# A two-layer conv/attention trunk: weight slots that mix blocks, vector work paced by counted time, every turn through DRAM

## The chip, the cores and the metric

One core of a Trainium2 chip runs one program. The metric is the device time of one execution in microseconds, as the median of several runs. PE is TensorE, DVE VectorE, ACT ScalarE, POOL GpSimd, SP SyncE; SP and POOL only issue DMAs here, apart from a few memsets.

## The reference

Two layers with the same structure on 256 positions of width 2048, all in float32. A layer norms x, multiplies it by one wide matrix, and splits the product between two branches; each branch is gated and projected, and the sum goes through an output projection onto x.

```python
def hybrid_layer(x, cos, sin, norm_g, w_in, ...):
    h = rmsnorm(x, norm_g)
    proj = h @ w_in
    (c_a, c_glu, c_gate, q_down, kv_down, k_pe, m_gate, g_conv, g_mla) = jnp.split(proj, idx, axis=-1)
    y_conv = conv_branch(c_a, c_glu, c_gate, conv_w, conv_b, conv_ln_g, conv_ln_b) @ w_proj_conv
    y_mla = mla_branch(q_down, kv_down, k_pe, m_gate, cos, sin, ...) @ w_proj_mla
    y = jax.nn.sigmoid(g_conv) * y_conv + jax.nn.sigmoid(g_mla) * y_mla
    return x + y @ w_out
```

The convolution branch is c_a * sigmoid(c_glu), a causal convolution of 31 taps in each of the 2048 channels, a layer norm over the channels, and two SiLU gates. The attention branch expands q_down and kv_down (512 wide) to 16 heads of 192 for queries and keys (128 plain, 64 rotated) and 128 for values, norms queries and keys per head, and attends with a mask of chunks of 64.

## The kernel before

**Products.** Every projection is cut into blocks of up to 512 output columns. `product` (line 289) runs a block as a row of slots. A slot takes one piece of weights, 2 x 128 input channels, and issues 12 matmuls: for both halves of the positions and both chunks, high x high, low x high and high x low, all fp32r, so that two rounded parts stand for one float32. SP loads a piece as `raw` (line 183), ACT rounds it to `hi` (line 194), DVE subtracts to get `lo` (line 210); `raw` has 5 buffers, `hi` 4, `lo` 3. A block of w_in has 8 slots, one of the query or key expansion (`uq`, `ukv`) 2. The results lie in `acc`, four banks of PSUM, two for each block that runs. They are evacuated one slot after the block's end (`EVAC_AT`).

**The order.** `order_of_layer` (line 89) lists a layer's blocks: a first gated block `glu`, the three blocks `down`, two more `glu`; then for each of 8 pairs of heads `uq`, `ukv` and one more `glu` or gate block; then the gates, the projections `pmla` and `pconv`, and `wout`. A block runs to its end before the next one starts. Everything else is placed against the running slot: `at_slot(n, f)` (line 223) issues f behind the n-th slot from now, and `late` behind the other work of the slot. The statistics, turns, scores, exponentials and values of a pair hang on `ukv` at fixed slots (lines 67 and 68: scores at 17, values at 32). `InOrder` (line 119) keeps each engine's instructions in the order of the calls.

**Fill.** The convolution's taps and its layer norm lie in a queue, `fill`. Behind each slot `background` (line 242) adds to a budget for DVE and ACT what the slot's matmuls leave beside the split, takes off the cost written beside each placed task, and issues fill while DVE's budget is positive. A tap is one addition of 128x512 where ACT has scaled the input beforehand (`scale`, line 839), else two multiply-adds of 128x256 (line 850). The costs are written by hand, such as `costs = (0.62, 0.0)`.

**Turns.** To move channels to the partitions, a block is written to DRAM in four parts by POOL (`park`, line 321), read back (`fetch`) four slots later, and transposed in squares of 32 by DVE at the eighth (`turn`, line 338). Only the last quarter of `pconv`, and of `wout` before another layer, is transposed by PE with an identity into the PSUM tile `tp` (`turn4`, line 986), as the next product needs it soon.

**The other PE work.** The scores `s` of a pair are 16 matmuls, the values `o_ps` 12 (line 781). The layer norm's mean `mu` and variance `var` are sums over the partitions by matmuls of plain F32 with a matrix of 1/2048 (lines 890 and 912); `mu` is issued a slot after the last tap was issued. The pair's statistics end in `rsqrt_steps` (line 369), a run of dependent instructions of 8 elements.

Of the kernel before, what the change touches and what calls it, by code (L numbers as in the profile page):

```python
# [12 lines left out]
F32 = mybir.dt.float32  # L13
# [7 lines left out]
P = 128  # L21
T = 2
# [35 lines left out]
KS = 2  # L58
N_WARM = 9
# [7 lines left out]
STATS_AT, SCALE_AT, QK_BACK_AT, QK_TURN_AT, NOPE_AT, ROPE_AT, SCORES_AT = 2, 3, 6, 11, 12, 14, 17  # L67
MAX_AT, EXP_AT, P_BACK_AT, P_TURN_AT, P_SPLIT_AT, VALUES_AT, O_AT = 18, 19, 23, 28, 30, 32, 34
# [20 lines left out]
def order_of_layer():  # L89

    order = [("glu", 0, "win")] + [("down", i, "win") for i in range(len(DOWN_BLOCKS))]
    order += [("glu", 1, "win"), ("glu", 2, "win")]
    for b in range(NPAIR):
        order += [("uq", b, "wuq"), ("ukv", b, "wukv")]
        if b + 3 < 8:
            order.append(("glu", b + 3, "win"))
        elif b + 1 < NPAIR:
            order.append(("cgate", b - 5, "win"))
    for kind, s in (
        ("cgate", "win"), ("mgate", "win"), ("gmla", "win"), ("pmla", "wpm"),  # L100
        ("gconv", "win"), ("pconv", "wpc"), ("wout", "wo"),
    ):
        order += [(kind, i, s) for i in range(2 if kind == "cgate" else 0, 4)]
    return order

# [10 lines left out]
def trunk(ctx: ExitStack, tc: tile.TileContext, xT, x, g_in, pos, win, wuq, wukv, wpc, wpm, wo, cst, rows, invf, out):  # L116
    nc = tc.nc

    class InOrder:


        def __init__(self, engine):
            self.engine, self.last = engine, None

        def __getattr__(self, name):
            def issue(*a, **k):
# [4 lines left out]
                self.last = ins.ins  # L131
                return ins
# [3 lines left out]
    pe, vec, act, gps, sp = (InOrder(e) for e in (nc.tensor, nc.vector, nc.scalar, nc.gpsimd, nc.sync))  # L136
# [14 lines left out]
    acc_p = pool("acc", 4, space=PSUM)  # L151
    tp_p = pool("tp", 2, space=PSUM)
# [5 lines left out]
    streams = {"win": (win, 16), "wuq": (wuq, 4), "wukv": (wukv, 4), "wpc": (wpc, 16), "wpm": (wpm, 16), "wo": (wo, 16)}  # L158
    taken = {}
    pieces = []  # L160

    def plan(layer, stream):
        ap, nk = streams[stream]
        i, at = taken.get((layer, stream), (0, 0))
        n = blocks_of_layer()[stream][i]
        mine = []
        for g in range(nk // KS):
            size = P * KS * n
            pieces.append((ap[layer, at : at + size].rearrange("(p k c) -> p k c", p=P, k=KS), n))
            at += size  # L170
            mine.append(len(pieces) - 1)
        taken[layer, stream] = (i + 1, at)
        return nk, n, mine


    plans = []
    for l in range(DEPTH):
        plans.append([(k, i, plan(l, s)) for k, i, s in order_of_layer()])
# [42 lines left out]
    fill, budget, marks, owed, assist = deque(), {"vec": 0.0, "act": 0.0}, {}, [], []  # L221

    def at_slot(ahead, f, vec=0.0, act=0.0):
        steps.append((clock[0] + ahead, (vec, act), f))

    def spend(costs):
        budget["vec"] -= costs[0]
        budget["act"] -= costs[1]

    def soon(f, vec=0.0, act=0.0):  # L230

        owed.append(f)
        at_slot(1, lambda: pay(f), vec, act)
# [8 lines left out]
    def background(n):  # L242
        clock[0] += 1
        slot = 12 * (n / 2400 + 0.0133) - 0.04
        for e, split_us in (("vec", KS * n / 960 + 0.06), ("act", KS * n / 1066 + 0.04)):
            budget[e] = min(budget[e], 0.0) + slot - split_us
        while True:
# [4 lines left out]
            for _, costs, f in due:  # L252
                spend(costs)
                f()
# [1037 lines left out]
```

## Time and profile before

| | |
|---|---|
| median of 3 runs | 1903.43 us (1903.39 to 1903.7) |
| span of the profiled execution | 1900.7 us, 2.7 below the median; its own time from outside was not recorded |
| busy PE / DVE / ACT / POOL | 99% / 84% / 70% / 21% |
| DMA | 441.91 MB, 232 GB/s in the mean |

How to read it: a row of groups gives line, engine, operation, out<-in, shape, count, then busy time, mean ns of one, and the idle time ahead of it with what ended it. All instructions go through one helper and show its line (L127), so tiles tell them apart. A row of waits gives who waited for whom, the total, the count and the longest. The chain of waits, followed back from the end, is shown in order of time. PE's busy time counts pipelined matmuls to their modelled ends, so the distance of starts is the better measure of their rate.

### The profile page before, as it was taken

Reading aid. Unit: us, or ns where it says so; the run is one execution under the profiler, and the core shown is the slowest. Engines: PE = TensorE matmul, PEld = TensorE weight load, DVE = VectorE, ACT = ScalarE, POOL = GpSimd, SP = SyncE. Lnnn points to the kernel's source line nnn. Section 1 sums busy time; section 2 is a strip of 40 time slices with the busy share of each in tenths; the row PEclk is TensorE's granted clock in tenths of the full one; section 3 lists DMA queues with packets and bytes.
Section 4 is the critical chain, followed back from the end, with each engine's and each line's share of the span. In section 5 each row is a group of like instructions: output and inputs, shape, how many; then the busy total and the mean of one; then the engine's idle time right before and its main releaser. Section 6 shows DMA issues by size and latency. Waiting matters only on the chain.

```text
span 1900.7 us, 27392 instructions
## 1 busy us (share of the span) xinstructions
PE 1886.3 (99%) x8753; PEld 1591.4 (84%) x8753; DVE 1601.6 (84%) x2620; ACT 1329.3 (70%) x2346; POOL 394.3 (21%) x734
## 2 busy tenths in 40 slices
PE   9999999999999999999999999999999999999999
PEld 7988888888888878888899888888888888788887
DVE  6899888899999998565669898988999999975654
ACT  6677887878788757444557688688887887574442
POOL 0143433332200000121211443343322000001200
PEclk9999999999999999999999999999999999999999
DMA  8777778776765566577866787887777555656764
GB/s 296 233 246 259 255 243 273 264 253 216 239 210 186 186 215 216 203 238 256 286 211 214 254 270 242 262 267 240 261 226 237 199 184 196 221 200 214 240 223 164
DMA packets 137376, 441.91 MB, mean 232 GB/s; under 512 B 23440, under 2 KB 27280, under 8 KB 137232
## 3 DMA queue, kind: packets, MB, share of 16 engines
q1 hardware_dynamic: 104688, 359.50, 55.3%
q0 software_dynamic: 31968, 80.26, 13.4%
q8 instruction: 68, 1.11, 0.2%
q14 instruction: 76, 0.62, 0.1%
q10 hardware_dynamic: 576, 0.41, 0.1%
HBM read 397.61 MB, written 42.47 MB: 232 GB/s over the span
## 4 chain that ended last, share of the span: by engine, by line
PE 94%; DVE 2%; DMA 1%; issue 1%; ACT 1%; SPq 0%; POOL 0%; DVEq 0%; ACTq 0%
PE acc L127 91%; PE s L127 2%; PE o_ps L127 1%; DVE lo L127 1%; DVE v_t L127 1%; DMA raw<-in_win 1%; DMA pos_t<-in_pos 0%; ACT hi L127 0%; SPq L127 0%; DVE qk L127 0%; PE tp L127 0%; DVE rsq_t L127 0%; DMA turn_d<-pr 0%; PE mu L127 0%; ACT junk L127 0%
## 5 line engine op out<-in xcount | busy, mean ns | idle before, releaser
L127 DVE TENSOR_TENSOR lo<-raw,hi 128x1024 fp32r<-128x1024 f32 (+3 forms) x689 | 812.3, 1182 | 214.9 <-PE acc L127 173.0
L127 ACT CAST hi<-raw 128x1024 fp32r<-128x1024 f32 (+3 forms) x689 | 699.3, 1022 | 413.1 <-PE acc L127 343.1
L127 PE MATMUL acc<-hi,hT 128*128 128x512 f32 (+2 forms) x1728 | 419.8, 382 | 0.0
L127 PEld LDWEIGHTS acc<-hi,hT 128*128 128x128 f32 x1728 | 319.7, 188 | 59.2
L127 ACT ACTIVATE tap<-u_t,cst 128x256 f32<-128x256 f32 x594 | 259.7, 500 | 20.5 <-DVE v_t L127 19.8
L127 PE MATMUL acc<-hi,h_hi 128*128 128x512 f32 (+2 forms) x864 | 261.6, 384 | 0.7 <-ACT hi L127 0.7
L127 PE MATMUL acc<-hi,h_lo 128*128 128x512 f32 (+2 forms) x864 | 261.1, 383 | 0.0
L127 PE MATMUL acc<-lo,h_hi 128*128 128x512 f32 (+2 forms) x864 | 230.4, 383 | 2.4 <-DVE lo L127 2.4
L127 PE MATMUL acc<-lo,hT 128*128 128x512 f32 (+2 forms) x864 | 229.3, 382 | 0.0
L127 DVE TENSOR_TENSOR v_t<-v_t,tap 128x512 f32<-128x512 f32 x297 | 204.2, 688 | 10.6 <-ACT tap L127 0.5
L127 PEld LDWEIGHTS acc<-lo,h_hi 128*128 128x128 f32 x864 | 160.8, 188 | 33.1 <-DVE lo L127 3.1
L127 PEld LDWEIGHTS acc<-hi,h_lo 128*128 128x128 f32 x864 | 161.7, 188 | 30.1
L127 PEld LDWEIGHTS acc<-hi,h_hi 128*128 128x128 f32 x864 | 160.8, 188 | 30.9 <-ACT hi L127 1.8
L127 PEld LDWEIGHTS acc<-lo,hT 128*128 128x128 f32 x864 | 160.5, 188 | 29.9
L127 POOL DMA_DIRECT2D turn_d<-gate x176 | 95.9, 553 | 342.9 <-DVE gate L127 298.6
L127 DVE SCALAR_TENSOR_TENSOR v_t<-u_t,cst,v_t 128x256 f32<-128x256 f32 x366 | 157.9, 481 | 3.2
L127 POOL DMA_DIRECT2D turned<-turn_d x82 | 46.0, 562 | 502.9 <-DVE v_t L127 162.4
L127 PE MATMUL acc<-hi,oT 128*128 128x512 f32 x512 | 128.1, 390 | 0.0
L127 PE MATMUL acc<-hi,yT 128*128 128x512 f32 x512 | 128.0, 389 | 0.0
L127 PE MATMUL acc<-hi,ycT 128*128 128x512 f32 x512 | 127.7, 389 | 0.0
L127 PE MATMUL acc<-hi,qkc 128*128 128x512 f32 (+1 forms) x512 | 119.1, 364 | 1.4 <-ACT junk L127 1.4
L127 PEld LDWEIGHTS acc<-hi,oT 128*128 128x128 f32 x512 | 96.1, 188 | 20.2
(166 smaller groups left out, 2143.8 us busy)
## 6 DMA issues: line engine op xcount, KB each, us to landing
raw<-in_win SPq DMA_DIRECT2D x383, 512.0 KB, 4.2
raw<-in_wpm SPq DMA_DIRECT2D x64, 512.0 KB, 3.2
raw<-in_wpc SPq DMA_DIRECT2D x64, 512.0 KB, 3.7
raw<-in_wo SPq DMA_DIRECT2D x64, 512.0 KB, 4.3
raw<-in_wukv SPq DMA_DIRECT2D x32, 512.0 KB, 5.3
turned<-turn_d POOLq DMA_DIRECT2D x50, 256.0 KB, 4.4
raw<-in_win SPq DMA_DIRECT2D x32, 384.0 KB, 4.5
raw<-in_wuq SPq DMA_DIRECT2D x32, 384.0 KB, 3.0
```

What stands on the lines that cost most here:

```text
L127: ins = getattr(self.engine, name)(*a, **k)
```

## The change

1. **Slots that mix blocks.** `slots_of_layer` lists single slots: each `uq` and `ukv` (2 slots each) stands inside a gate block (3 slots of it, `uq`, 2 slots, `ukv`, 3 slots). Blocks 0 and 1 of `pconv` and `wout`, and in layer 1 the first `glu` with the first `down`, run in turns of two slots. Weight pieces are loaded in that order. PSUM has two fixed pairs of banks, handed on when a block ends.
2. **Pace by counted time.** The budgets and hand-written costs go. Every instruction issued on PE, DVE and ACT adds a time by its shape to a counter; at each slot the counters of DVE and ACT are raised to PE's, and fill runs while DVE's is over 0.4 us behind PE's.
3. **Turns by DRAM alone.** `turn4`, the identity and `tp` go.
4. **PE work.** The values take high and low part of the probabilities in one matmul of 512 columns, and end in two banks that ACT copies and DVE adds. Mean and variance first add their two halves, split the sum into two fp32r parts, and take two matmuls.
5. **DVE and ACT.** Small steps of the statistics are woven between large DVE instructions. Taps by addition and the sum `s1` are split in two halves. The gate's first factor is scaled by ACT, and the product issued a slot later. Several `late` tasks move a slot on.
6. **Places.** Scores at 20, values at 34; the rope tables compute five slots later, and their loads come one slot earlier; the first `mgate` tile is turned 6 slots after its evacuation, the last `cgate` tile is parked 2 slots later; x for `wout` is loaded three slots before a block's end. The first chunk of x and the gains come as one tile.

```diff
+STREAM_K = {"win": NCT, "wuq": LORA // P, "wukv": LORA // P, "wpc": NCT, "wpm": NCT, "wo": NCT}
...
-STATS_AT, SCALE_AT, QK_BACK_AT, QK_TURN_AT, NOPE_AT, ROPE_AT, SCORES_AT = 2, 3, 6, 11, 12, 14, 17
-MAX_AT, EXP_AT, P_BACK_AT, P_TURN_AT, P_SPLIT_AT, VALUES_AT, O_AT = 18, 19, 23, 28, 30, 32, 34
+STATS_AT, SCALE_AT, QK_BACK_AT, QK_TURN_AT, NOPE_AT, ROPE_AT, SCORES_AT = 2, 5, 9, 14, 15, 17, 20
+MAX_AT, EXP_AT, P_BACK_AT, P_TURN_AT, P_SPLIT_AT, VALUES_AT, O_AT = 21, 22, 25, 28, 31, 34, 36
...
+        if kind in ("pconv", "wout") and i == 0 or layer and kind == "glu" and i == 0:
+            for j in range(0, slots[b], 2):
+                out += [(b + a, j + e) for a in range(2) for e in range(2)]
+            b += 2
+        elif b + 1 < len(order) and order[b + 1][0] == "uq":
+            out += [(b, 0), (b, 1), (b, 2), (b + 1, 0), (b + 1, 1), (b, 3), (b, 4), (b + 2, 0), (b + 2, 1)]
+            out += [(b, 5), (b, 6), (b, 7)]
+            b += 3
...
+    now = {"pe": 0.0, "vec": 0.0, "act": 0.0}
+    def pe_us(name, dst, lhs, rhs, **_):
+        return (rhs.free_size() + 32) / 2400
+    def vec_us(name, dst, *a, **_):
+        if name == "tensor_copy":
+            return dst.free_size() / 1920 + 0.08
+        n = dst.free_size() if name != "tensor_reduce" else a[0].free_size()
+        if n <= 8:
+            return 0.19
+        return n / 960 + (0.13 if name == "scalar_tensor_tensor" and not isinstance(a[1], float) else 0.07)
...
+    def weave(dst):
+        if woven and not weaving and dst.shape[0] == P and dst.free_size() >= 128:
+            weaving.append(1)
+            if next(woven[0], woven) is woven:
+                woven.popleft()
+            weaving.pop()
+    vec.after = weave
...
-        while fill and budget["vec"] > 0:
+        while fill and now["vec"] < now["pe"] - 0.4:
             after, slots, scalar = fill[0][1]
-            if after and clock[0] < marks.get(after, 1 << 30) + slots or scalar and budget["act"] < 0:
+            if any(clock[0] < marks.get(a, 1 << 30) + slots for a in after) or scalar and now["act"] > now["pe"]:
                 break
             run_fill()
-        while assist and budget["act"] > 0.8 and assist[0]():
-            budget["act"] -= 0.85
+        while assist and now["act"] < now["pe"] - 0.8 and assist[0]():
+            pass
...
+        for e in ("vec", "act"):
+            now[e] = max(now[e], now["pe"])
...
             def values():
-                st["o"] = tp_p.tile([P, 2, SEQ], F32, tag="tp", name="o_ps")
+                st["o"] = o_p.tile([P, 2, 2, SEQ], F32, tag="o", name="o_ps")
...
+                    pe.matmul(o, v[0][:, 0, h, :], A.pt[:, :, h, past], start=True, stop=False)
+                    pe.matmul(o[:, 0, P:], v[1][:, 1, h, :], A.pt[:, 0, h, own], start=False, stop=False)
+                    pe.matmul(o[:, 0, :], v[1][:, 0, h, :], A.pt[:, 0, h, past], start=False, stop=False)
+                    pe.matmul(o[:, :, P:], v[0][:, 1, h, :], A.pt[:, :, h, own], start=False, stop=True)
...
+                act.copy(o, st["o"][:, :, 0, :])
+                at_slot(1, lambda: vec.tensor_add(o, st["o"][:, :, 1, :], o))
...
+            act.activation(u, ps[:, :256], AF.Copy, scale=r)
...
-                vec.scalar_tensor_tensor(u, ps[:, :256], r, sg, op0=ALU.mult, op1=ALU.mult)
+                vec.tensor_mul(u, u, sg)
...
-                    vec.tensor_add(v[:, :, :SEQ], v[:, :, :SEQ], scaled.pop(k))
+                        vec.tensor_add(vj, vj, own[:, j])
...
-                for j in range(2):
-                    pe.matmul(st["mu"], ones, s1[:, j, :], start=j == 0, stop=j == 1)
+                    for n, part in enumerate(st["parts"]):
+                        pe.matmul(st[name], ones, part, start=n == 0, stop=n == 1)
...
-            then(mean, after=("s1", 7), slots=1)
+            then(mean_sum, after=(("s1", 7),))
+            then(mean, after=(("mean", "parts"),), slots=2)
...
-            if c < 3:
-                return turn(src, 512, None, then=use, then_costs=costs)
...
-                    pe.transpose(tps[0][:, j].rearrange("p i s -> p (i s)"), src[:, j * P : (j + 1) * P], ident)
...
-            turn4(evac_src, c, use, 0.65, 0.65)
+            turn(evac_src, 512, None, then=use)
...
-            late.append(normalised)
+            at_slot(1 if c else 6, normalised)
...
-                        at_slot(a + 2, lambda: next(tables, None), 0.0 if a < 2 else 0.95)
+                        at_slot(a + (1 if a < 2 else 7), lambda: next(tables, None))
...
+            if blk.kind == "wout" and j == blk.nk // KS - 3:
+                wout_begin(blk.i)
```

Three places show what moves. PE, the values of the first pair in layer 0, before; `pv` holds the probabilities and values as they are split, `qk_t` more of the same.

```order
L127 MATMUL o_ps<-pv_1402 128x256
L127 MATMUL o_ps<-pv_1402 128x128 x3
L127 MATMUL o_ps<-pv_1402 128x256 x3
L127 MATMUL o_ps<-pv_1402 128x128 x3
L127 MATMUL o_ps<-pv_1402 128x256 x2
```

PE at the same place now.

```order
L169 MATMUL o_ps<-pv_1523 128x512
L169 MATMUL o_ps<-pv_1523 128x128
L169 MATMUL o_ps<-pv_1523 128x256
L169 MATMUL o_ps<-pv_1523 128x2x128
L169 MATMUL o_ps<-pv_1523 128x512
L169 MATMUL o_ps<-pv_1523 128x128
L169 MATMUL o_ps<-pv_1523 128x256
L169 MATMUL o_ps<-pv_1523 128x2x128
```

Twelve matmuls of 2304 columns in all have become eight of 2304.

DVE, the statistics of a pair of layer 0, before: `ss_p` sums of squares, `r_p` the factors, `rsq_t` a helper.

```order
L127 TENSOR_TENSOR lo_3123<-raw_2963,hi_3087 128x1024
L127 TENSOR_TENSOR ss_p<-ss_p,ss_d 128x4
L127 TENSOR_SCALAR ms<-ss_p 128x8
L127 TENSOR_SCALAR rsq_t<-ms 128x8
L127 TENSOR_SCALAR r_p<-rsq_t 128x8
L127 TENSOR_TENSOR rsq_t<-r_p 128x8
L127 SCALAR_TENSOR_TENSOR rsq_t<-rsq_t,ms 128x8
L127 SCALAR_TENSOR_TENSOR r_p<-rsq_t,r_p 128x8
```

DVE at the statistics of the same pair now.

```order
L169 TENSOR_TENSOR ss_p<-ss_p,ss_d 128x4
L169 SCALAR_TENSOR_TENSOR v_t<-u_t,cst,v_t 128x256
L169 TENSOR_SCALAR ms<-ss_p 128x8
L169 SCALAR_TENSOR_TENSOR v_t<-u_t,cst,v_t 128x256
L169 TENSOR_SCALAR rsq_t<-ms 128x8
L169 TENSOR_TENSOR lo_3381<-raw_3248,hi_3354 128x1024
L169 TENSOR_SCALAR r_p<-rsq_t 128x8
L169 RECIPROCAL rinv<-sums 128x2x2
L169 STREAM_TRANSPOSE pr<-pr 128x768
L169 TENSOR_TENSOR rsq_t<-r_p 128x8
```

The dependent small steps, one run before, now stand one by one behind large instructions; the rest of the run follows closed up, ahead of the scaling of the keys.

PE, the mean of layer 1, before: the two matmuls of `mu` follow the slot of `lo_16312`.

```order
L127 MATMUL acc_0_16290<-lo_16312,oT_14461 128x512 x2
L127 MATMUL acc_1_16291<-lo_16312,oT_14461 128x512 x2
L127 MATMUL mu<-s1c,ones 128x256 x2
L127 MATMUL acc_0_16290<-hi_16314,oT_14461 128x512 x2
L127 MATMUL acc_0_16290<-hi_16314,oT_14462 128x512 x2
```

DVE at that place, before: the last tap and `s1c` stand behind `lo_16337`, which belongs to the slot after it.

```order
L127 TENSOR_TENSOR lo_16312<-raw_16185,hi_16294 128x1024
L127 TENSOR_TENSOR v_t<-v_t,tap 128x2x256 x2
L127 SCALAR_TENSOR_TENSOR v_t<-u_t,cst,v_t 128x256 x2
L127 TENSOR_TENSOR lo_16337<-raw_16212,hi_16314 128x1024
L127 TENSOR_TENSOR v_t<-v_t,tap 128x2x256
L127 TENSOR_TENSOR s1c<-s1c,v_t 128x512
```

DVE there now: the sum's low half `tot` stands behind `lo_16898`, and PE takes `mean` behind the slot of `lo_16898`.

```order
L169 TENSOR_TENSOR s1c<-s1c,v_t 128x256 x2
L169 TENSOR_TENSOR lo_16838<-raw_16713,hi_16818 128x1024
L169 STREAM_TRANSPOSE turned<-turned 128x512 x2
L169 TENSOR_TENSOR lo_16858<-raw_16747,hi_16840 128x1024
L169 TENSOR_TENSOR ln_stats<-s1c 128x256
L169 TENSOR_TENSOR lo_16877<-raw_16767,hi_16860 128x1024
L169 TENSOR_TENSOR lo_16898<-raw_16795,hi_16879 128x1024
L169 TENSOR_TENSOR tot<-ln_stats,tot 128x256
```

What PE's matmul reads stood one row of `lo` behind the slot it follows; it now stands right behind that slot's own `lo`.

More of the change, by code (lines that the diff above doesn't have):

```diff
@@ L287, in order_of_products, with slot_of @@
         return [e for t in two for p in two for e in high(t, p)] + low(0) + low(1)
-    def product(planned, stat, evacuate, evac_at=EVAC_AT, costs=(0.0, 0.0), before=None):
-        nk, n, mine = planned
-        pts = [acc_p.tile([P, 512], F32, tag="acc", name=f"acc{mine[0]}_{t}") for t in range(T)]
+    banks = [0, 1]
+    def slot_of(blk, j):
+        last = blk.nk // KS - 1
+        if j == 0:
+            blk.bank = banks.pop(0)
+            blk.pts = [
+                acc_p.tile([P, 512], F32, tag=f"acc{blk.bank}{t}", name=f"acc{blk.mine[0]}_{t}") for t in range(T)
+            ]
@@ L317, in stat_of @@
+        if j == last:
+            banks.append(blk.bank)
+            steps.insert(0, (clock[0] + 1 + blk.evac_at, evac))
+        background()
     def stat_of(hi, lo):
```

465 lines of the change are left out of this document (250 added, 215 removed).

## The prediction

> **What bounds the kernel now.** I read the page's busy shares first, then PE's waits, then the chain of waits in order of time, and last the vector engine's waits and busy time by stage. The first line gives the span, the second the busy time of each engine.
>
> ```profile
> span 1900.7 us, 27392 instructions
> PE 1886.3 (99%) x8753; PEld 1591.4 (84%) x8753; DVE 1601.6 (84%) x2620; ACT 1329.3 (70%) x2346; POOL 394.3 (21%) x734
> ```
>
> PE is busy for 1886.3 of 1900.7 us, so TensorE's own instruction stream sets the time, and only two things can move it: fewer or shorter instructions on PE, and less waiting in front of them. The idle rest is 14.4 us. The view of waits says what PE waited for:
>
> ```profile
> PE mu L127 <- DVE s1c L127: 3.1, 1, 3.1
> PE acc L127 <- DVE lo L127: 2.6, 3, 1.9
> PE acc L127 <- ACT junk L127: 1.4, 1, 1.4
> PE acc L127 <- ACT hi L127: 0.7, 2, 0.4
> PE s L127 <- DVE qk_t L127: 0.7, 1, 0.7
> ```
>
> The 0.7 on hi lies at the start. The other four, 7.8 us together, lie in the middle. Some 4 us of the rest is the tail behind the last product. The chain in order of time (start, length, engine and tile) gives the price of every piece of PE's work:
>
> ```profile
> 33.88 6.64 DMA pos_t<-in_pos
> ...
> 152.96 6.15 DMA raw<-in_win
> ...
> 181.83 31.45 PE acc L127 x144
> 213.29 1.89 PE s L127 x16
> ...
> 223.36 1.37 PE o_ps L127 x12
> ...
> 694.59 0.86 PE mu L127 x4
> 695.46 21.80 PE acc L127 x96
> 717.26 0.86 PE var L127 x4
> ...
> 870.49 0.87 PE tp L127 x8
> ...
> 1621.76 1.10 PE mu L127 x4
> ...
> 1647.36 0.86 PE var L127 x4
> ...
> 1814.19 0.87 PE tp L127 x8
> ...
> 1896.73 0.42 DVE xres L127
> ```
>
> One pair of heads is 144 slot matmuls, the scores s and the values o_ps: 31.45 + 1.89 + 1.37 = 34.7 us of PE. Sixteen such pairs run, eight in each layer.
>
> **The change on PE.** The slot matmuls are the same number with the same columns, in another order, so their cost stays. Three things shrink.
>
> *Values.* Before, a pair has 12 matmuls of 256 and 128 columns, 2304 columns in all; now 8, again 2304 columns. What a matmul costs beside its columns comes from the rows: a matmul of 512 columns takes 21.80 / 96 = 0.227 us, and the 24 matmuls of 384 columns in the group of 144 are left with 31.45 - 120 x 0.227 = 4.2 us, 0.175 each, so a column is 0.052 / 128 = 0.41 ns. The 16 score matmuls have 3840 columns (1.57 us) and take 1.89: 20 ns each beside the columns. The 12 of the values have 0.945 us of columns and take 1.37: 35 ns each. Four fewer, with the rest at 20 to 35 ns, leave 1.10 to 1.23 us, and I take 1.17: 0.20 us a pair, 3.2 us over 16 pairs (2.2 to 4.2). The Trainium skill, page "TensorE: Matmul & The Clock Gate", section "Wait — 56ns, not 53.3ns?", puts the fixed cost of a matmul at about 2.5 ns; by that rule 64 fewer matmuls would be worth an estimated 0.16 us, not 3.2. The rows of this case speak for the larger figure, since 12 short matmuls take 0.4 us more than their columns.
>
> *Mean and variance.* The four groups take 0.86 + 0.86 + 1.10 + 0.86 = 3.7 us, each showing four matmuls where the program has two (the operands are plain F32). They become two fp32r matmuls of 256 columns, the kind that makes up the scores at 1.89 / 16 = 0.12 us each: 0.24 us a group, 0.95 in all. 2.7 us less; I count 2.5, as the 1.10 holds some of the wait ahead of it.
>
> *Transposes.* Three groups of tp (two are in the rows, 0.87 us each) go: 2.6 us.
>
> PE's work falls by 3.2 + 2.5 + 2.6 = 8.3 us (7.3 to 9.5).
>
> **The waits that go.** The 3.1 on mu is an ordering fault: the order puts the two mu matmuls of layer 1 one slot ahead of the DVE instruction that ends s1c. Now PE's matmul follows only two slots after the low part of the sum is marked as issued, so the wait goes, unless DVE is over a slot behind. Of the 2.6 on lo, 1.9 comes from the rope tables, which DVE starts before the positions have landed (6.64 us); the tables now start five slots later and their DMA one slot earlier, so it goes. The other 0.7 of it lies at the overloaded end of the convolution, as does most of DVE's lateness, and goes too. The scores now stand three slots later behind the pair, but no further behind their split, so the 0.7 on qk_t may stay; I count it as gone, since the last rows of the split are no longer ahead of a run of small dependent steps. The 1.4 on junk follows a weight transfer of 6.15 us; that can come back anywhere, and I count half. Gone: 3.1 + 2.6 + 0.7 + 0.7 = 7.1 us. The start stays: the new single tile for the first chunk lands at best some 0.4 us earlier, but the second weight piece gates PE right behind it.
>
> **What is added, and beside what it lies.** On DVE a convolution tap by addition becomes two halves, the values get an addition, the gate's product reads SBUF; more taps are scaled on ACT. The stage to watch is that of the pairs. Per-stage busy time (PE, PEld, DVE, ACT, POOL, PE clock, DMA) for two pairs of layer 0, and for two stages between the pairs and the layer's mean:
>
> ```profile
> 252.00:321.00 69.00, 69.00 (x343) 59.28 (x342) 60.79 (x125) 57.37 (x128) 27.81 (x52) 1.00 0.76 254
> 525.00:590.00 65.00, 65.00 (x288) 53.81 (x288) 63.39 (x94) 53.96 (x91) 0.57 (x1) 1.00 0.57 199
> 1515.00:1580.00 65.00, 65.00 (x289) 53.72 (x288) 63.36 (x96) 51.41 (x89) 0.00 (x0) 1.00 0.52 185
> ```
>
> The groups with their busy time and mean:
>
> ```profile
> L127 DVE TENSOR_TENSOR v_t<-v_t,tap 128x512 f32<-128x512 f32 x297 | 204.2, 688 | 10.6 <-ACT tap L127 0.5
> L127 DVE SCALAR_TENSOR_TENSOR v_t<-u_t,cst,v_t 128x256 f32<-128x256 f32 x366 | 157.9, 481 | 3.2
> L127 DVE SCALAR_TENSOR_TENSOR su<-acc,rinv_x,su 128x256 f32<-128x256 f32 x32 | 13.9, 476 | 11.0 <-ACT su L127 11.0
> L127 DVE TENSOR_TENSOR v_t<-turned,v_t 128x256 f32<-128x256 f32 x32 | 11.7, 419 | 0.3
> L127 DVE TENSOR_TENSOR o_sb<-turned,o_sb 128x512 f32<-128x512 f32 x16 | 11.1, 692 | 0.6
> L127 ACT ACTIVATE su<-acc,rinv_x 128x256 f32<-128x256 f32 x32 | 13.4, 470 | 4.3 <-DVE rinv_x L127 4.2
> ```
>
> DVE has 60.79 us in 69.0, which is 30.6 a pair. In the program's order a pair's twelve slots hold two whole additions and four halves by scalar before, four half additions and ten halves by scalar now: by busy time over count, 2 x 0.688 + 4 x 0.431 = 3.1 becomes 4 x 0.366 + 10 x 0.431 = 5.8. The addition for o_sb is 0.69, the gate's product falls by 2 x (0.434 - 0.366) = 0.1. DVE comes to 30.6 + 2.7 + 0.7 - 0.1 = 33.9 of now 34.5 us a pair. That is 98%, and PE hides it only if DVE hardly waits. Between pairs and mean DVE is at 63.4 of 65 us (97.5%) with PE at 65.00: so full a DVE costs PE nothing by itself. What DVE waits for in the pairs of layer 0:
>
> ```profile
> DVE lo L127 <- ACT hi L127: 6.5, 5, 1.4
> DVE su L127 <- ACT su L127: 4.9, 4, 1.5
> DVE pv L127 <- ACT junk L127: 4.2, 6, 1.0
> DVE lo L127 <- issue: 2.4, 4, 1.3
> ```
>
> 18.0 us over eight pairs, 2.3 a pair. The 4.9 on su goes, as the product is issued a slot after ACT's part: 1.65 stays, against 0.6 of room. These are waits of an engine that comes early, in front of ACT; a later DVE waits less by as much. So I take most of them to shrink, and count 2.0 us of new PE waiting over the 16 pairs, from a range of 0 to 9. ACT gains two scalings of 256 a pair (0.47 us each, as the su row) beside 57.37 of 69: it has room. In the stage up to the mean the work that is moved into the pairs is missing, so DVE falls below its 97.5% there.
>
> *Turns by DRAM alone.* The last quarter of the projections leaves PE and takes POOL's queue: eight writes, two reads. It lies beside the first 12 slots of the next product, which now runs two blocks in turns and needs that quarter only then:
>
> ```profile
> turned<-turn_d POOLq DMA_DIRECT2D x50, 256.0 KB, 4.4
> turn_d<-xres POOLq DMA_DIRECT2D x24, 64.0 KB, 4.5
> L127 POOL DMA_DIRECT2D turn_d<-gate x176 | 95.9, 553 | 342.9 <-DVE gate L127 298.6 <-ACT gate L127 40.0 <-issue 4.3
> ```
>
> A slot is 12 x 0.227 = 2.72 us, 12 slots are 32.7. The evacuation on DVE (four instructions of 512 elements at 0.69, as the o_sb row), eight writes of 0.55, their landing of 4.5 and the read of 4.4 with two issues come to some 17 us; the program places the turn 8 slots on (21.8 us) and the split by ten slots (27.9 us with its own 0.7). Nothing is exposed, with some 5 us of cover; if a transfer took over 5 us more, PE would wait for the excess in three places. The first gate's late tile, the late parking of the last gate and the later loads of x lie on queues with room, and cost nothing behind the same cover.
>
> **The sum.** 1903.43 - 8.3 - 7.1 + 2.0 = 1890.0 us. The profiled execution has a span of 1900.7, 2.7 below the median of the runs; I carry that offset unchanged.
>
> **The rivals.**
>
> *The waits come back elsewhere* (0.14). PE gains its 8.3 us, but DVE at 98% in the pairs lets PE wait about as long as now: 1903.43 - 8.3 is 1895. For it: PE already waits for qk_t in a pair. Against: the longest waits of now are faults of order.
>
> *DVE becomes the bound in the pairs* (0.14, the half of it slower than before). Place: the split of the weights' low part and the scores' split, behind DVE's longer queue. If none of the 1.65 us a pair shrinks, a pair takes 33.9 + 1.65 = 35.55 against 34.5, 1.05 more, 16.8 us in all, which eats the gain of 15.4: 1905. If ACT's added 0.94 us a pair comes on top as further waiting, it is 2.0 a pair, 32 us: 1920. It decides at 15.4 / 16 = 0.96 us of PE waiting a pair. For it: the counted time leaves out every wait for another engine. Against it: the rows of 97.5%.
>
> *Each DVE instruction costs its whole length* (0.02). There are 342 more of them on DVE, some 72 in a pair against 62 (half of the x125 of the window). The timeline below shows the next one starting 0.08 us before the one ahead has ended. Without that, a pair would take 33.9 + 72 x 0.08 = 39.7 us against 34.5, 83 us in all: some 1971. Against it: by the same count the kernel before would need 30.6 + 62 x 0.08 = 35.6 a pair, and it takes 34.7.
>
> ```profile
> 537.27 0.70 DVE L127 STREAM_TRANSPOSE turned<-turned 128x512 f32<-128x512 f32 x1
> 538.01 0.69 DVE L127 TENSOR_TENSOR o_sb<-turned,o_sb 128x512 f32<-128x512 f32 x1
> 538.62 1.22 DVE L127 TENSOR_TENSOR lo<-raw,hi 128x1024 fp32r<-128x1024 f32 x1
> 539.75 0.70 DVE L127 STREAM_TRANSPOSE turned<-turned 128x512 f32<-128x512 f32 x1
> ```
>
> The lo of 1.22 us is followed after 1.13, the product of 0.69 after 0.61; only the product that reads what the transpose wrote starts after its end. That dependent tail is what halves hide. The Trainium skill, page "VectorE: DVE Perf Modes", section "The DRAIN you can't avoid", says that the next instruction waits until the pipe is empty; it would make halves a loss. The trace agrees for dependent neighbours alone.
>
> **Chances.** The forecast, 1886 to 1895, has 0.70; the waits that come back 0.14 (to 1900); DVE as the bound 0.14; whole lengths 0.02. A measurement of this kernel can tell about 0.2%, 3.8 us, from no change. Faster by more: 0.70 + 0.14 + 0.01 = 0.85. Within: 0.08. Slower: 0.05 + 0.02 = 0.07. The low end, 1885.5, takes 9.5 us off PE and all 7.8 of the waits with none new, and a start 0.4 earlier: 1885.7. The high end, 1900, takes 7.3 off PE, 5 off the waits and 9 of new ones: 1900.1. That leaves out the 0.16 of the last two rivals.
>
> **What would show it.** Right: 8 matmuls of o_ps in about 1.17 us, mean and var in 0.24, no tp, no wait on mu or mean, DVE over 95% busy in the pairs' stage, PE's idle time some 9 us in all. Wrong: a wait of PE for lo or qk_t that comes back in every pair, by more than 0.5 us; PE waits in the first slots of wout or of layer 1 for a turned quarter; or a median above 1900.

## The result and the profile after

The changed kernel takes 1879.6 us in the median (1879.24 to 1880.43, 4 runs), the kernel before 1903.57 (1903.39 to 1906.16, 4 runs): a ratio of 0.9871 with a 95% interval of 0.9857 to 0.9885, 24 us faster. The forecast was 1890.0 with a low end of 1885.5. The sign was right, the size too small by 10 us.

The page of the changed kernel, its span and the engines' busy time:

```profile
span 1878.1 us, 27952 instructions
PE 1871.6 (100%) x8657; PEld 1582.9 (84%) x8657; DVE 1611.9 (86%) x2962; ACT 1378.9 (73%) x2482; POOL 408.4 (22%) x762
```

The whole list of what PE waited for:

```profile
PE warm L169 <- DVE zeros L169: 1.5, 1, 1.5
PE acc L169 <- ACT hi L169: 1.0, 1, 1.0
```

Both lie in the first 10 us (`warm` are matmuls on zeros ahead of the first product). Of the four waits in the middle, nothing is left. In the chain of waits, PE's own work ahead of and behind the first values, and the two matmuls of mean and variance in layer 1:

```profile
195.35 1.90 PE s L169 x16
...
230.56 5.47 PE acc L169 x24
236.02 1.16 PE o_ps L169 x8
237.18 25.97 PE acc L169 x120
...
1617.80 0.24 PE mean L169 x2
1618.04 35.38 PE acc L169 x156
1653.42 0.24 PE var L169 x2
```

Eight matmuls of the values take 1.16 us where twelve took 1.37; mean and variance take 0.24; tp does not occur. Per-stage rows, two pairs of layer 0 and the stage ahead of the mean (window and its length, busy time of PE, PEld, DVE, ACT and POOL, then granted clock, DMA share and GB/s):

```profile
267.30:336.30 69.00, 69.00 (x338) 59.40 (x337) 65.69 (x143) 59.34 (x132) 27.41 (x51) 1.00 0.82 267
...
560.00:625.00 65.00, 65.00 (x288) 53.83 (x288) 62.05 (x121) 57.14 (x102) 0.00 (x0) 1.00 0.58 193
```

DVE is busy for 65.69 of 69 us in the pairs (95%, from 88%), and PE does not wait once. Ahead of the mean DVE went the other way, from 97.5% to 95%.

**Where the 22.6 us of span went.** I measured PE by the distances of its matmuls' starts. In the traces of before and after, 97% of the slot matmuls keep within 5 ns of (columns + 32) / 2400 us, which is 0.227 us for 512 columns, 0.173 for 384 and 0.147 for 320. What a distance has beyond that is lost time, whether the view of waits shows it or not.

| part | forecast, us | distances show, us |
|---|---|---|
| values, 12 to 8 matmuls | 3.2 | 3.4 |
| mean and variance, with the matmul slowed behind each | 2.5 | 2.6 |
| transposes by PE | 2.6 | 2.6 |
| wait of mu | 3.1 | 3.3 |
| wait for the rope tables | 1.9 | 3.8 |
| waits for lo ahead of the mean | 0.7 | 2.9 |
| waits for qk_t, ahead of and inside the scores | 0.7 | 2.1 |
| wait behind ACT's `junk` | 0.7 | 1.6 |
| new waits | -2.0 | 0 |
| start and the rest | 0 | 0.3 |

PE's work was forecast well, 8.3 against 8.6. The waits were not: 5.1 net against 14.0. (`junk` is the unused output of ACT's sums of squares, which read `acc`.) The remaining 1.4 us of the medians' difference are offsets: the span of before lies 2.9 below its median, that of the changed kernel 1.5.

### The profile page after: what moved, and what is told of

It reads as the page before. It is cut to its first block, busy times and chain, and to the rows that moved or that the text cites. A ratio compares the mean times of both kernels' runs of the same rounds, so it can differ in the third digit from the quotient of the medians.

```text
span 1878.1 us, 27952 instructions
## 1 busy us (share of the span) xinstructions
PE 1871.6 (100%) x8657; PEld 1582.9 (84%) x8657; DVE 1611.9 (86%) x2962; ACT 1378.9 (73%) x2482; POOL 408.4 (22%) x762
## 4 chain that ended last, share of the span: by engine, by line
PE 99%; DMA 0%; SPq 0%; ACT 0%; DVE 0%; issue 0%; DVEq 0%
PE acc L169 97%; PE s L169 2%; PE o_ps L169 1%; DMA raw<-in_win 0%; SPq L169 0%; ACT hi L169 0%; PE var L169 0%; PE mean L169 0%; DVE xres L169 0%; DVEq L1388 0%
## 5 line engine op out<-in xcount | busy, mean ns | idle before, releaser
L169 ACT ACTIVATE tap<-u_t,cst 128x256 f32<-128x256 f32 x694 | 300.1, 500 | 16.6 <-DVE v_t L169 13.0
L169 DVE TENSOR_TENSOR v_t<-v_t,tap 128x256 f32<-128x256 f32 x694 | 250.4, 418 | 0.2
L169 POOL DMA_DIRECT2D turn_d<-gate x192 | 104.3, 551 | 318.1 <-DVE gate L169 251.8
L169 DVE SCALAR_TENSOR_TENSOR v_t<-u_t,cst,v_t 128x256 f32<-128x256 f32 x266 | 114.6, 479 | 0.0
L169 PEld LDWEIGHTS acc<-hi,yT 128*128 128x128 f32 x512 | 96.1, 188 | 20.0
```

Source lines behind the costliest of these rows:

```text
L169: ins = getattr(self.engine, name)(*a, **k)
```

## Experiments on the kernel before

Four edits, each alone, on one chip; before took 1905.29 us there (26 runs, 1900.4 to 1908.3). A trace is one execution out of this spread: that of before is one of the shorter ones, with a span of 1900.7 where the median of the 26 is 1903.5. So the times are compared by medians, and a trace is asked only for where its time goes.

**Rope tables moved.**

```diff
-at_slot(a + 2, lambda: next(tables, None), 0.0 if a < 2 else 0.95)
+at_slot(a + (1 if a < 2 else 7), lambda: next(tables, None), 0.0 if a < 2 else 0.95)
```

> The kernel before, with only the rope tables moved: their loads one slot earlier, their computing five slots later. In the trace of before, PE loses 2.04 us at 44.24 us and then runs its next ten matmuls of 384 columns in 0.32 instead of 0.175 us each, with a granted clock of 0.51 from 46.5 to 50.0. Theory A (a wait costs more than its idle time): the whole 3.9 us goes, 2.04 + 0.25 + 1.5, so 3.9 us off the kernel before, and the clock is 1.00 in that stretch. Rival B (my prediction's step: a wait is worth the 1.9 us that the view of waits shows): 1.9 us off. Rival C: the tables press on the vector engine elsewhere, under 1 us off.

1905.39 us (1903.66 to 1907.11, 11 runs), ratio 1.0002 (0.9993 to 1.0011): no gain at all. In the traced execution the wait at 44 us did go, but others stand in its place. Waits of PE in this run:

```profile
PE mu L127 <- DVE s1c L127: 5.3, 2, 3.1
PE acc L127 <- ACT junk L127: 4.0, 2, 2.0
```

mu now waits in layer 0 too, and junk in both layers. Rival C had the size, under 1 us, and theories A and B fell. That the tables press on DVE, as Rival C has it, is not shown, and a trace of one execution does not tell waits that follow from the move from waits that come and go.

**Mean two slots later.**

```diff
-then(mean, after=("s1", 7), slots=1)
+then(mean, after=("s1", 7), slots=3)
```

> The kernel before, with only the two matmuls of the mean issued two slots later. Theory A (a fault of order): the 3.3 us ahead of mu in layer 1 go, with the 0.2 us of slower matmuls behind it: 3.4 us off, nothing else moves. Rival B (the vector engine is late by its amount of work): the matmuls no longer wait, but the layer norm behind them starts 5.4 us later and PE waits for lo or for the convolution's output instead: under 1 us off.

1898.95 us (12 runs), ratio 0.9973 (0.9964 to 0.9982), 3 to 7 us off; the span is 4.4 shorter than in the trace of before, 3.3 of it the wait of mu. Theory A by its mechanism: mu no longer waits, and no wait grew in its place by more than 0.5 us. Its 3.4 us are the low end of what the medians show.

**One count changed.**

```diff
-                    costs = (0.62, 0.0)
+                    costs = (0.70, 0.0)
```

> The kernel before, with one number changed: a tap by addition is counted at 0.70 us instead of 0.62. In the timeline of before two additions in a row take 1.40 to 1.52 us. Theory A (the pace was counted wrong): the vector engine's lead over PE, 4.2 us at 510 us and 0.5 us at 640 us, holds above 2 us, and the waits for lo between 639 and 695 us (2.9 us) and at 1600 to 1612 us (0.4 us) go: 2.5 to 3.3 us off; mu still waits. Rival B (too much work before the mean, whatever the pace): the taps that are put off meet the layer norm, and PE waits in the first slots of the convolution's projection: no gain, or up to 3 us slower.

1892.22 us (1890.6 to 1892.62, 5 runs), ratio 0.9932 (0.9916 to 0.9948): 13 us off, more than half of the whole change, four times what I expected. Theory A had the mechanism, but it was too small, and mu was to go on waiting. All of PE's waits in this run:

```profile
PE acc L127 <- DVE lo L127: 1.9, 1, 1.9
PE warm L127 <- DVE zeros L127: 1.6, 1, 1.6
PE acc L127 <- ACT hi L127: 0.6, 2, 0.4
PE acc L127 <- DVE su L127: 0.5, 1, 0.5
```

mu, qk_t and junk do not wait any more, though none was touched. The 1.9 is that of the rope tables. The last matmul starts 9.9 us earlier than in the trace of before, as much as the table's rows for mu, lo, qk_t and junk make together; the rest of the 13 us is mostly the short execution that was traced of before. So the wait of mu was no fault of order by itself: DVE was late there because its slots had been filled past PE's time. What the count is measured on, in the timeline of DVE of before (start, length, what):

```profile
642.96 1.22 DVE L127 TENSOR_TENSOR lo<-raw,hi 128x1024 fp32r<-128x1024 f32 x1
644.09 1.48 DVE L127 TENSOR_TENSOR v_t<-v_t,tap 128x512 f32<-128x512 f32 x2
645.61 0.88 DVE L127 SCALAR_TENSOR_TENSOR v_t<-u_t,cst,v_t 128x256 f32<-128x256 f32 x2
```

Two additions take 645.61 - 644.09 = 1.52 us, where the pace counted 1.24. Between the gates and the mean (slots 200 to 224) the old kernel issued 2.16 taps a slot, this one 2.0. DVE's lead is the time from the end of a slot's `lo` to the start of the first matmul that reads it; its lowest at slots 228 to 252 of layer 0 went from 0.05 us to over 4.

The count has a second effect. ACT scales at most two taps ahead of DVE, so taps that are issued later are more often found scaled: 321 of 480 here, 297 before. A scaled tap takes DVE less (0.69 us against 2 x 0.43), and the run does not tell this from the fuller slots.

**Taps by addition in halves.**

```diff
-                    vec.tensor_add(v[:, :, :SEQ], v[:, :, :SEQ], scaled.pop(k))
+                    own = scaled.pop(k)
+                    for j in range(2):
+                        vec.tensor_add(v[:, j, :SEQ], v[:, j, :SEQ], own[:, j])
```

> The kernel before, with each tap by addition split in two of 256 columns, as in the changed kernel. In the traces two whole additions take 1.40 us up to the next lo, four halves 1.34. Theory A (the halves hide the tail of a dependent instruction): 0.03 us a tap, 0.06 us a slot; the lead falls by 0.02 a slot instead of 0.08 on the way to the mean, and the 2.9 us of waits for lo go: 2 to 3 us off. Rival B (busy time decides: two halves are 0.72 us, a whole one 0.69): the lead falls faster, 0.5 to 3 us slower.

1897.72 us (9 runs), ratio 0.9965 (0.9954 to 0.9976), 4 to 9 us off. The waits for lo ahead of the mean and those of mu went, with the same number of taps a slot; junk waited longer instead (4.6 us in all) in the traced execution, the slowest of the nine. Theory A has the mechanism, with 2 to 3 us too small a size. The changed kernel's halves, four of them up to the next lo:

```profile
582.60 1.42 DVE L169 TENSOR_TENSOR v_t<-v_t,tap 128x256 f32<-128x256 f32 x4
583.94 1.22 DVE L169 TENSOR_TENSOR lo<-raw,hi 128x1024 fp32r<-128x1024 f32 x1
```

1.34 us for two taps, where the old kernel needs 1.40 to 1.52: so little a tap is enough.

**The count and the rope tables together.**

> The kernel before with the tap counted at 0.70 us (alone that gave 1892.2) and with the rope tables moved as in the changed kernel (alone that gave nothing: the wait at 44 us went, but waits of 2.2 and 2.4 us stood in other places). Theory A (where the pace is right the other waits do not come back): the 2.06 us at 44.08 us and the 1.6 us of half clock behind it go, 3.7 us: about 1888.5. Rival B (what is gained early is lost later, as in the run alone): about 1892.

1888.36 us (1888.23 to 1890.0, 4 runs), ratio 0.9918 (0.9905 to 0.9932), on another chip, where before took 1903.93: theory A to 0.2 us. The move that alone was worth nothing is worth 3.9 us by the medians once the pace is right, or 2.7 by the ratios to before on each chip; in the traces the 3.7 us at 44 us are gone. PE's waits in this run are those of the start:

```profile
PE warm L127 <- DVE zeros L127: 1.6, 1, 1.6
PE acc L127 <- ACT hi L127: 1.0, 2, 0.7
```

1888.4 less the 8.6 us of PE's work is 1879.8, where the changed kernel has 1879.6; in the traces the last matmuls start 8.3 us apart. By this sum two lines of the old kernel and PE's shorter work account for the whole change. No run has just these three together, and the sum does not say that the rest of the change is worth nothing in the changed kernel.

**Why a wait of 1.9 us cost 3.8.** Per-stage rows of before around the rope tables; the third figure from the end is the granted clock:

```profile
44.20:46.50 2.30, 0.42 (x4) 0.10 (x2) 2.13 (x9) 1.52 (x4) 0.00 (x0) 1.00 0.25 96
46.50:50.00 3.50, 3.50 (x11) 3.50 (x12) 3.29 (x12) 2.55 (x5) 2.04 (x4) 0.51 0.46 131
50.00:52.00 2.00, 2.00 (x13) 2.00 (x13) 1.90 (x6) 0.83 (x1) 2.00 (x5) 1.00 0.85 241
```

Behind the wait the clock stands at 0.51 for 3.5 us. PE is busy in all of it, so the view of waits has nothing; but nine of its eleven matmuls stand 0.32 us apart and not 0.173. By the distances the wait is 2.0 us and the eleven matmuls lose 1.7, with 0.1 beside them: 3.8. (The expectation for the rope tables' run adds its three terms to 3.9; they make 3.8.)

## Experiments on the changed kernel

These were measured on three chips, on which before took 1903.9 to 1904.5 us in the median. The changed kernel's 1879.6 was not measured again beside them, so a difference of 1 or 2 us is not well told from one between chips.

**A low count alone.**

```diff
+        if name == "tensor_add":
+            return n / 960 + 0.03
```

> The changed kernel, with an addition counted at 0.04 us less: 0.297 instead of 0.337 us for 256 columns, so 0.08 less for a tap, which is the error of the kernel before (0.62 counted against 0.70). All work and all places are those of the changed kernel. Theory A (the true count of the pace is what removed the waits): the vector engine's lead falls again on the way to the mean, and waits for lo, qk_t or the mean come back: 2 to 7 us slower than the changed kernel. Rival B (the new places, the weaving and the mixed slots removed them): within 1 us of the changed kernel.

1879.15 us (1878.99 to 1879.36), ratio 0.9866 (0.9851 to 0.9881): rival B; theory A fell. The lowest lead in the pairs of layer 0 went from 2.0 to 1.5 us, and taps ahead of the mean stayed at 2.0 a slot: with room of 1.58 us and a margin of 0.4, both counts stop after the second tap. The low count does so by little: two taps come to 1.187 us where 1.183 are left. By the count alone, an error a little larger would let a third tap in.

**The margin alone undone.**

```diff
-        while fill and now["vec"] < now["pe"] - 0.4:
+        while fill and now["vec"] < now["pe"]:
```

> The changed kernel without the margin of 0.4 us alone: taps are issued until the true count of the vector engine reaches PE's. Too low a count alone gave 1879.2, both together 1899.1. Theory A (the count decides, and the margin only covers it): a slot is filled up to PE's time by a true count, as in the kernel before with 0.70, where no wait for lo was left: within 2 us of the changed kernel's 1879.6. Theory B (the margin decides: what the count leaves out, 0.6 us of the vector engine's waits for others in a pair, has no room without it): waits for lo in the pairs and ahead of the mean, 5 to 15 us slower.

1881.19 us (1880.84 to 1881.62), ratio 0.9877 (0.986 to 0.9893): theory A, 1.6 us slower. The lowest lead in the pairs of layer 0 is 0.1 us, and 2.2 taps a slot are issued at slots 200 to 224.

**Both.**

> The changed kernel with both halves of the old pace: an addition counted 0.04 us too low (0.08 a tap; alone that changed nothing), and taps issued until the count reaches PE's, without the 0.4 us of margin, so that a slot is filled up by the count: by count 2.66 taps a slot ahead of the mean, which take 1.78 us beside 1.13 for the split, 2.91 in a slot of 2.72. Theory A (the waits of before came from slots filled past PE's time): the lead of 5.3 us falls to nothing ahead of the mean and waits for lo come back there and in the pairs: 5 to 12 us slower than the changed kernel. Rival B (places, weaving and mixing removed them): within 1.5 us.

1899.14 us (1898.78 to 1899.43, 8 runs), ratio 0.9973 (0.9962 to 0.9983): 19.5 us slower, beyond the 5 to 12 that I had worked out. PE's waits, and the stage ahead of the mean:

```profile
PE acc L171 <- DVE lo L171: 7.5, 13, 2.0
...
PE s L171 <- DVE qk_t L171: 0.2, 1, 0.2
```

```profile
540.00:620.00 80.00, 79.74 (x350) 65.12 (x349) 79.93 (x159) 68.40 (x123) 1.10 (x2) 1.00 0.55 189
```

DVE is busy for 79.93 of 80 us, with 2.4 taps a slot at slots 200 to 224. The view of waits shows 7.7 us of the 19. By the distances, a wait of 2.2 us and the slow matmuls behind it lose 3.9, another wait 2.1, and most of the rest lies in some 25 places of 0.15 to 1.2 us, in the pairs and ahead of the mean. Places, mixing and weaving are those of the changed kernel: pace alone makes or loses 19.5 us. True count or margin, either is enough here; without both, waits for lo are back.

The pace works in two ways here too. Taps that come early find less of ACT's scaling done, and DVE does them in two multiply-adds. First the changed kernel, then this run:

```profile
L169 DVE TENSOR_TENSOR v_t<-v_t,tap 128x256 f32<-128x256 f32 x694 | 250.4, 418 | 0.2
L169 DVE SCALAR_TENSOR_TENSOR v_t<-u_t,cst,v_t 128x256 f32<-128x256 f32 x266 | 114.6, 479 | 0.0
```

```profile
L171 DVE TENSOR_TENSOR v_t<-v_t,tap 128x256 f32<-128x256 f32 x550 | 198.7, 419 | 0.1
L171 DVE SCALAR_TENSOR_TENSOR v_t<-u_t,cst,v_t 128x256 f32<-128x256 f32 x410 | 176.3, 480 | 0.0
```

Scaled taps fall from 347 to 275 of 480, which is 10 us more of DVE's busy time. How much of the 19.5 us this makes, beside slots filled too far, was not tried apart. Without the margin alone 300 were scaled, and that run lost 1.6 us.

| pace of the changed kernel | margin 0.4 us | no margin |
|---|---|---|
| true count | 1879.6 | 1881.2 |
| 0.08 us a tap too low | 1879.2 | 1899.1 |

**More work in the pairs, not counted.**

```diff
+            def more_work():
+                parts = [h_hi[:, k, :].bitcast(F32) for k in (0, 1)]
...
+                for _ in range(2):
+                    vec.tensor_add(extra, *parts)
...
+            for a in range(4):
+                at_slot(3 * a + 1, more_work)
```

> The changed kernel with eight more vector additions of 256 columns in each pair of heads (their result is not used), which the pace does not count. By its trace the vector engine is busy 264.9 of 276 us over eight pairs, 33.1 of 34.5 a pair; eight additions of 0.36 us make 36.0. Theory A (DVE binds at 100%): 1.5 us a pair over, less the lead of some 5 us that a layer can use up: 7 us a layer, 14 us slower than the changed kernel (8 to 18). Rival B (the forecast's rival, in which DVE already costs PE time in pairs at 96 to 98%): all 36.0 - 33.1 = 2.9 us a pair show, 46 us slower.

1905.49 us (1905.06 to 1905.91, 11 runs), ratio 1.0006 (0.9997 to 1.0015): 26 us slower, between the two theories. Waits, and two pairs between equal points of the order:

```profile
PE acc L169 <- DVE lo L169: 13.8, 11, 2.2
```

```profile
264.11:337.43 73.32, 70.21 (x337) 59.31 (x337) 71.97 (x161) 59.04 (x132) 31.68 (x60) 1.00 0.77 246
```

A pair takes 73.32 / 2 = 36.7 us with DVE busy for 36.0: it binds at 98%, not at 100%, as DVE stays idle for 0.7 us a pair, in pieces that the view of waits does not list. The changed kernel's 33.1 with the same 0.7 is 33.8 of 34.5, so by this estimate the room is 0.7 us a pair. The rival of the forecast, a pair bound by DVE, was this near.

**The same work, counted.**

> The same eight additions in each pair, but counted by the pace like every other instruction. Theory A (the pace puts taps off for as long as DVE is full): 23 us of taps a layer move behind the pairs, where DVE has 5 of 65 us free at 560 to 625 us and 9 of 65 behind that; no wait in the pairs, and 0 to 6 us slower than the changed kernel. Rival B (the pace is only a fine adjustment): as slow as without the count, 8 to 18 us.

1932.1 us (1932.05 to 1932.26), ratio 1.0144 (1.0131 to 1.0158): 52 us slower, twice as bad as uncounted. Both theories missed. Stage of the pairs, and PE's waits:

```profile
184.00:460.00 276.00, 276.00 (x1332) 236.02 (x1331) 268.40 (x572) 232.24 (x487) 103.71 (x192) 1.00 0.78 257
```

```profile
PE acc L169 <- ACT ycT L169: 37.6, 8, 9.8
```

In the pairs the pace did what theory A said: no wait. But the taps that it put off made the convolution's output late. Its first high parts on ACT, here and in the changed kernel:

```profile
775.04 1.12 ACT L169 CAST ycT<-v_t 128x512 fp32r<-128x512 f32 x2
```

```profile
742.21 1.14 ACT L169 CAST ycT<-v_t 128x512 fp32r<-128x512 f32 x2
```

The projection that reads them starts at 766 us in the changed kernel, and here at 776. The fill has a deadline that the pace does not know, and PE pays there in eight waits up to 9.8 us, with slow matmuls behind them (a granted clock of 0.50 from 775.8 to 781.0).

**Values in twelve matmuls.**

```diff
-                    pe.matmul(o, v[0][:, 0, h, :], A.pt[:, :, h, past], start=True, stop=False)
...
+                    todo = [(0, 0, 0), (1, 0, 0), (1, 1, 0), (1, 0, 1), (0, 1, 0), (0, 0, 1)]
...
-                at_slot(1, lambda: vec.tensor_add(o, st["o"][:, :, 1, :], o))
```

> The changed kernel with the values again in 12 matmuls of 256 and 128 columns into one bank, without the second half's addition on DVE (0.69 us a pair). Theory A (a short matmul costs some 20 to 40 ns beside its columns): by the distances of starts the o_ps groups of before take 21.9 us in all and those of the changed kernel 18.5, so 3.4 us slower. Rival B (only the columns cost, which are the same 2304): no difference, below 0.5 us. Rival C (DVE's saved 0.69 us a pair is worth something): less than 3 us slower.

1882.39 us (1882.09 to 1882.46), ratio 0.9883 (0.987 to 0.9897): 2.8 us slower by the medians. That alone would also fit Rival C. The trace decides: the values take 3.4 us more, the start happens to wait 1.1 less, and no other wait of PE is there in either kernel for DVE's saved time to remove. Four short matmuls of the same total columns are worth 0.2 us: theory A.

**No weaving.**

```diff
-    vec.after = weave
```

> The changed kernel with the statistics' small steps in one run behind each other, not woven between large instructions. In the trace a step of 8 elements starts 0.20 us after the one that it depends on, and a woven one takes 0.05 to 0.07 of DVE's time; some five of a pair's steps are woven, so DVE has 0.65 us more a pair. With eight more additions a pair took 36.65 us at 36.0 us of work, so DVE needs its work and 0.6 us; 33.1 + 0.65 + 0.6 = 34.4 of 34.5. Theory A (that sum): 0 to 2 us slower than the changed kernel. Rival B (the weaving is what carries the pairs): waits for lo or qk_t in each pair, over 5 us.

1885.26 us (1884.99 to 1885.4), ratio 0.99 (0.9886 to 0.9913): 5.7 us slower, by waits in the first two pairs of each layer only (up to 1.3 us for lo and 0.3 for qk_t); Rival B has the size, but the waits are not in each pair. The steps in a run:

```profile
223.87 0.15 DVE L169 TENSOR_TENSOR ss_p<-ss_p,ss_d 128x4 f32<-128x4 f32 x1
224.06 0.17 DVE L169 TENSOR_SCALAR ms<-ss_p 128x8 f32<-128x8 f32 x1
224.26 0.17 DVE L169 TENSOR_SCALAR rsq_t<-ms 128x8 int32<-128x8 int32 x1
```

And woven, in the changed kernel:

```profile
217.55 0.17 DVE L169 TENSOR_SCALAR ms<-ss_p 128x8 f32<-128x8 f32 x1
217.63 0.17 DVE L169 RECIPROCAL rinv<-sums 128x4 f32<-128x4 f32 x1
...
218.59 0.13 DVE L169 TENSOR_SCALAR rsq_t<-ms 128x8 int32<-128x8 int32 x1
218.63 0.68 DVE L169 TENSOR_TENSOR qk_t<-qk,qk_t 128x512 fp32r<-128x512 f32 x1
```

A step that depends on the one ahead holds DVE for 0.20 us, an independent one lets the next start after 0.04 to 0.08. The Trainium skill, page "VectorE: DVE Perf Modes", section "The DRAIN you can't avoid", says that the next instruction does not start until the pipe is empty, and adds that one which is not held starts earlier. The rows show the first for dependent steps, and an earlier start for the others.

**Blocks not mixed.**

```diff
-            out += [(b, 0), (b, 1), (b, 2), (b + 1, 0), (b + 1, 1), (b, 3), (b, 4), (b + 2, 0), (b + 2, 1)]
-            out += [(b, 5), (b, 6), (b, 7)]
+            out += [(b + 1, 0), (b + 1, 1), (b + 2, 0), (b + 2, 1)] + [(b, j) for j in range(8)]
```

> The changed kernel with the query and key blocks ahead of the gate block, not inside it: the four short slots stand together again, ahead of eight of the gate. Theory A (the mixing spreads the short slots and the transfers): around the first pairs a weight piece lands in 6 to 8 us instead of 3 to 5.5, and waits of PE behind ACT's junk of 1.5 to 2.8 us come back in one or both layers, some with slow matmuls behind: 2 to 6 us slower than the changed kernel. Rival B (the pace removed those waits too, as in the kernel before with 0.70): within 1 us.

1881.03 us (1880.54 to 1881.74), ratio 0.9878 (0.9865 to 0.9892): 1.4 us slower. The long waits behind junk did not come back, only losses of 0.2 us behind ACT in three pairs. Theory A fell, and the time lies just outside Rival B's 1 us: the mixing is worth little here.

## Why the prediction was wrong

**PE's work: right.** 8.3 forecast, 8.6 measured, the values' term confirmed by the run with twelve matmuls.

**"Gone: 3.1 + 2.6 + 0.7 + 0.7 = 7.1 us": the sizes were wrong.** They were read from the view of waits, which has only the time in which PE is idle. The rope tables' 1.9 had another 1.7 us of slow matmuls behind it. A matmul of 512 columns is shown for 0.389 us, and the next starts after 0.227, so a delay of up to 0.16 us, as for lo and inside the scores, is not idle time at all. By distances the same list is worth some 14 us. The low end of the range carried this fault, since it took "all 7.8 of the waits".

**"Count 2.0 us of new PE waiting": wrong, there is none.** DVE did go to 95% in the pairs, near the 98% forecast, but the room of 0.7 us a pair was enough.

**The step behind both: the pace was left unweighed.** The sum has no term for counted time. I treated the change from written costs to counted time as a matter of place, and looked for a cause for each wait: "an ordering fault", "the overloaded end of the convolution". The runs showed one cause for most of them. The count of 0.62 for what takes 0.70 to 0.76 filled slots to 2.16 taps, and DVE's lead fell by some 0.08 us a slot until whatever came next had to wait. One number takes 13 us off the kernel before; both halves of the old pace put 19.5 us on the changed one. A wait can have several cures: mu's also went with its place alone, and those of lo and mu with the taps in halves.

**The rivals.** "The waits come back elsewhere" fits the rope tables' move in the old kernel, which gave nothing, but not the new pace. "DVE becomes bound in the pairs" was close: eight short additions more a pair would have made it true.

**"Nothing is exposed" for the turns: right.** PE's list of waits has nothing behind a turned quarter.

**Left open.** Why the unwoven steps cost PE in the first two pairs of a layer and not later was not tried. How much of the pace's worth goes through the taps that ACT scales was not tried either. And why junk's wait goes with the right count is open. A late weight piece does not explain it: there the piece at that place was issued at 151.06 us and not at 152.96, but it landed no earlier (159.2 against 159.1 us), and ACT rounds it and reads `acc` behind it within 0.2 us of the same times. PE at this place, before and with the right count:

```profile
161.52 1.19 PE L127 MATMUL acc<-hi,qkc 128*128 128x512 f32 x4 [1.36 <-ACT junk L127]
```

```profile
158.90 2.01 PE L127 MATMUL acc<-hi,qkc 128*128 128x512 f32 x8
```

Before, PE's fifth matmul of the slot waits until ACT has read `acc`; with the right count it follows at once.

## What to carry to other kernels

Measure a bound engine by the distances of its instructions' starts: the view of waits showed 7.8 us where some 14 were to be had. Where work is fitted into the gaps of another engine by a count, check the count against the timeline first: a tenth too little on one instruction cost 13 us. Keep a margin, which cost nothing here. Such a fill needs its deadline in view too: work that was put off for the sake of one stage came 33 us later than in the changed kernel, and the next stage started 9 us late.

## What was not expected of the hardware

A wait of PE of about 2 us is sometimes followed by some 3 us at half the granted clock. It was behind waits of 1.9, 2.0 and 2.1 us (by the distances) at 44 us in three kernels, and of 2.2 us in layer 1 of the run with the rope tables moved:

```profile
1100.00:1103.00 3.00, 1.18 (x6) 0.66 (x4) 3.00 (x5) 2.08 (x7) 1.39 (x3) 1.00 0.86 273
1103.20:1106.30 3.10, 3.10 (x7) 2.48 (x8) 1.43 (x2) 2.11 (x8) 2.65 (x5) 0.50 0.82 289
```

It was not behind 1.5 us, behind another 2.2 in the same run, or behind the 3.3 of mu. The Trainium skill, page "TensorE: Matmul & The Clock Gate", section "Part 1: The HAM clock gate (the "warmup" mystery)", lets the clock fall after an idle window of some 3.4 us that runs freely; the 3 us of half clock and the chance in it fit, but here waits of 1.9 us were enough. The kernel before spread over 8 us in 26 runs and the changed one over 1.2 in 4. That waits of this kind make the spread is not shown: the run with the extra work counted has slow matmuls behind most of its long waits and spread over only 0.2 us in 4.
